# Two-layer decoder on one core: the retention output product with its four plain chunks first

## The chip, the core and the metric

The kernel runs on one core of a Trainium2 chip. The time is the device time of one execution in microseconds (us); the kernel before takes 1469.75 us in the median of three runs (1469.37 to 1470.0). Engines are called as in the profile: PE multiplies matrices (PEld is its loading of weights), DVE is the vector engine, ACT the scalar engine, POOL the general one, SP the one whose queue issues nearly all DMAs.

## The reference, cut to what matters

```python
D_MODEL = 1024; SEQ = 512; DEPTH = 2; RET_HEADS = 4; RET_V_DIM = 256; D_FF = 4096

def hybrid_layer(x, ...):
    z = rmsnorm(x, g_mix) @ w_in            # q, k, v of attention and retention, gates
    ya = sliding_window_sink_attention(aq, ak, av, sinks) @ w_a
    r = chunkwise_retention(rq, rk, rv)
    r = r * lax.rsqrt(jnp.mean(r * r, axis=-1, keepdims=True) + EPS)   # norm of each head
    r = r.reshape(B, S, RET_V) * jax.nn.silu(rg)
    yb = r @ w_b                            # the retention output product, 1024 x 1024
    mixed = sigmoid(ga) * ya + sigmoid(gb) * yb
    x = x + mixed @ w_out                   # 1024 x 1024
    x = x + square(relu(rmsnorm(x, g_mlp) @ w_up)) @ w_down
    return x

x = hybrid_layer(x, ...)                    # twice
return rmsnorm(x, g_final)
```

Everything is fp32. The input is one sequence of 512 tokens.

## The kernel before

**Products.** Activations lie transposed: 128 channels on the partitions, 512 tokens along them. Each fp32 operand is held as two values `hi` and `lo` whose sum it is, and each product is three matmuls (`products`): `hi` by `hi` (L332), weight `hi` by activation `lo` (L333), weight `lo` by activation `hi` (L334). ACT makes `hi` by a copy and DVE makes `lo` by a subtraction, L286 and L287 for weights, L339 and L340 for activations (`split`; L342 and L343 with a scale).

**Weights.** They come as units of 128x1024, in the one order that `unit_order` lists. SP's queue loads a unit into one of three `raw` buffers; ACT and DVE split it into one of three `hi` and `lo` buffers. So `raw` of a later unit is loaded only once DVE has split an older one, and a new `hi` waits until PE has used the older one for the last time.

**Chunks.** A chunk is 128 output channels by 512 tokens in one PSUM bank. A plain chunk takes 24 matmuls of 128x512. A `group` works on four chunks in four banks with the input blocks in the outer loop (96 matmuls, 4 units), `two_chunks` on two banks (48 matmuls, 2 units).

**Block pairs.** `narrow_pair` makes two chunks by a block scheme with fewer multiplications: 4 units (parts), 96 matmuls of 128x256, on sums of the activations' quarters. `sum_input` makes these sums for two pairs of input blocks: four DVE operations of 128x512 (L626, L627, L629, L630) and two splits of 128x1024 into the buffers called `r` (4 activations stacked; `r<-sums` in the profile). A pair's own DVE work is L675 and L678 (adding a partial result out of PSUM) and three calls of its `put`. PSUM banks are reused inside a pair: its last quarter is written into the bank that L675 reads, so it waits for L675. Two further DVE operations for each pair of weights that was not prepared earlier make the weights' sums (L252, L255, L259, L260).

**Stage around the change.** The retention output product (`w_b`) comes in this order: pair 0 and pair 2 (`mixed_pair`, L1238; `put` multiplies by the gate at L1244, and L1247 adds the attention's part for both chunks), then `sum_input` over the first half of the mixed values, then four plain chunks, each evacuated by `put_mixed` (L1218 multiplies, L1219 adds, then a split), then `sum_input` over the second half. In between, `delayed_step` lets one delayed split be issued at steps 2 and 4 of a pair. Then the residual `x` is loaded anew (L1278) into the buffer that held the attention's part, and the product with `w_out` follows: `two_chunks` (L1306; each adds into `x` at L1288) and three pairs (L1296). `next_input` scales and splits the finished chunks of `x` for the product after it (L342, L343).

**Last head.** Each retention head has a norm over 256 channels. Heads 0 to 2 go through `inverse_rms_apart`, head 3 through `inverse_rms` (square root on ACT at L479, reciprocal of 128x512 on DVE at L480). `finish` multiplies by the inverse and by the gate (L1089, L1090), per 128x512.

**What sets the order.** The kernel is written in Tile's language, with `schedule_with_timeline_sim=True`: a planner sets each engine's order of instructions from its own estimate of when their inputs are there. Each engine then works strictly in that order, so an instruction that waits holds up all behind it on its engine.

Of the kernel before, what the change touches and what calls it, by code (L numbers as in the profile page):

```python
# [14 lines left out]
ALU = mybir.AluOpType  # L15
# [3 lines left out]
P = 128  # L19
# [39 lines left out]
def unit_order():  # L59

    def plain(name, *at):
        return [(name, i) for i in range(*at)]

    def pairs(src, *firsts):
        return [("pair", j, part, src) for j in firsts for part in range(4)]

    order = plain("w_in", 26) + plain("w_a", 4) + plain("w_in", 26, 46)
    order += pairs("w_b", 0, 2) + plain("w_b", 4, 8)
    order += plain("w_out", 2) + pairs("w_out", 2, 4, 6)
    for what, q, i in mlp_sequence():  # L70
        if what == "first":
            order += plain("w_up", 4)
        elif what == "pair":
            order += pairs("w_up", 8 * q + 2 * i)
        elif what == "down":
            order += plain("w_down", 8 * q + 2 * i, 8 * q + 2 * i + 2)
        else:
            order += plain("w_down", 8 * q, 8 * q + 8)
    return order
# [43 lines left out]
def view(slot):  # L123
    return slot[0][:, slot[1], :]
# [3 lines left out]
def decoder(ctx, tc, xT, x_first, w_in, w_a, w_b, w_out, w_up, w_down, tables, decay, band, triangles, g_last, out):  # L128
# [207 lines left out]
    def split(hi, lo, src, scale=None):  # L336

        if scale is None:
            nc.scalar.activation(hi, src, AF.Copy)  # L339
            nc.vector.tensor_tensor(lo, src, f32(hi), ALU.subtract)  # L340
        else:
            nc.scalar.activation(hi, src, AF.Copy, scale=scale)  # L342
            nc.vector.scalar_tensor_tensor(lo, src, scale, f32(hi), ALU.mult, ALU.subtract)  # L343
# [259 lines left out]
    def layer_body(layer):  # L603
# [6 lines left out]
        def forms_home():  # L610

            t = slots.four()
            form = t[0].rearrange("p a (b t) -> p (a b) t", t=H).rearrange("p (j k s) t -> p j k s t", k=2, s=2)
            return t, form

        def sum_input(by_form, b, ks):

            (b11, b12), (b21, b22) = ((t[:, :, :H], t[:, :, H:]) for t in b)
            f = [big("sums").rearrange("p a (b t) -> p (a b) t", t=H) for _ in range(2)]
            t1, t2, t3, t4 = f[0][:, 0:2, :], f[0][:, 2:4, :], f[1][:, 0:2, :], f[1][:, 2:4, :]  # L620

            def parts_of_forms(j):
                t = by_form[2 * (j // 2) + ks // 2]
                return [t[:, :, :, s, :] for s in range(2)]

            nc.vector.tensor_tensor(t1, b12, b11, ALU.subtract)  # L626
            nc.vector.tensor_tensor(t2, b22, t1, ALU.subtract)  # L627
            split(*parts_of_forms(0), f[0].rearrange("p (j k) t -> p j k t", k=2))
            nc.vector.tensor_tensor(t3, b22, b12, ALU.subtract)  # L629
            nc.vector.tensor_tensor(t4, b21, t2, ALU.subtract)  # L630
            split(*parts_of_forms(2), f[1].rearrange("p (j k) t -> p j k t", k=2))
# [10 lines left out]
        def form_of(by_form):  # L642
            return lambda j: [by_form[2 * (j // 2) + k // 2][:, j % 2, k % 2, :, :] for k in range(4)]
# [7 lines left out]
        def narrow_pair(pool, step, form, block, put):  # L651
            def multiply(ps, weights, left, moving, start=True):
                hi, lo = weights
                cols = [slice((0 if left else 4 * P) + k * P, (0 if left else 4 * P) + (k + 1) * P) for k in range(4)]
                pairs = [((hi[:, c], lo[:, c]), m if isinstance(m, tuple) else (m[:, 0, :], m[:, 1, :])) for c, m in zip(cols, moving)]
                products(ps, pairs, start, True, not start)

            b, a, e = (bank(pool, "mm")[:, :H] for _ in range(3))
            eu, z = temp("eu"), big("z")
            part = unit("pair", layer)  # L660
            multiply(a, part, True, block(0, 0))
            ins = nc.scalar.activation(b, a, AF.Copy).ins
            step(ins)
            multiply(e, part, False, form(0))
            ins = nc.scalar.activation(eu[:, :H], e, AF.Copy).ins
            step(ins)
            part = unit("pair", layer)
            multiply(b, part, True, form(1), False)
            ins = nc.scalar.activation(eu[:, H:], b, AF.Copy).ins
            step(ins)  # L670
            multiply(a, part, False, block(1, 0), False)
            step(put(0, FIRST, a, z).ins)
            part = unit("pair", layer)
            multiply(b, part, True, form(2), False)
            ins = nc.vector.tensor_tensor(z[:, 1, SECOND], b, eu[:, :H], ALU.add).ins  # L675
            step(ins)
            multiply(e, part, False, block(1, 1), False)
            ins = nc.vector.tensor_tensor(z[:, 0, SECOND], e, eu[:, H:], ALU.add).ins  # L678
            step(ins)
            part = unit("pair", layer)  # L680
            multiply(b, part, True, form(3), False)
            put(slice(0, 2), SECOND, z[:, :, SECOND], z)
            put(1, FIRST, b, z)
            return z
# [324 lines left out]
        class Head:  # L1009
# [70 lines left out]

            def norm(self):
                self.inv = temp("inv")
                (inverse_rms if self.h == 3 else inverse_rms_apart)(self.parts, RET_V, self.inv)

            def finish(self):
                h = self.h
                for e in range(2):
                    z = rg.pop(2 * h + e)
                    nc.vector.tensor_tensor(z, z, self.inv, ALU.mult)  # L1089
                    nc.vector.tensor_tensor(z, self.rr[e], z, ALU.mult)  # L1090
                    hi, lo = slots.one(), slots.one()
                    split(view(hi), view(lo), z)
                    ret[2 * h + e] = (hi, lo)

        def retention(pair):
# [104 lines left out]
        def gate_tile():  # L1200
            c = len(gates)
            two = big("gate")
            nc.sync.dma_start(two, aside[:, c : c + 2, :])
            gate_tiles.append(two)
            gates.extend(two[:, j, :] for j in range(2))
# [18 lines left out]
        rT = [tuple(view(s) for s in ret[k]) for k in range(KD)]  # L1224
        delayed = []

        def delayed_step():
            turn = iter(range(6))

            def step(ins):  # L1230
                now = next(turn)
                if now in (2, 4) and delayed:
                    with tc.issue_after(ins):
                        delayed.pop(0)()

            return step

        def mixed_pair(c):  # L1238

            gate_tile()  # L1240
            two, own = gate_tiles[c // 2], CROSSED[c]

            def put(i, at, src, z):
                return nc.vector.tensor_tensor(two[:, i, at], two[:, i, at], src, ALU.mult)  # L1244

            narrow_pair(ps_aux if c == 0 else ps_mm, delayed_step(), form_of(by_form_r), block_r, put)
            nc.vector.tensor_tensor(two, two, x[:, own : own + 2, :], ALU.add)  # L1247
            delayed.extend(partial(split_mixed, c + i, gates[c + i]) for i in range(2))

# [1 line left out]
            at = slice(tokens * H, tokens * H + H)  # L1251
            return [tuple(m[:, at] for m in rT[CROSSED[k]]) for k in range(4 * half, 4 * half + 4)]

        for c in (0, 2):
            mixed_pair(c)
        all_of(delayed)
        delayed.clear()
        for t, _ in homes_r:
            slots.give(*t[1])
        homes_m = [forms_home(), None, forms_home(), None]  # L1260
        by_form_m = [h and h[1] for h in homes_m]
        sum_input(by_form_m, gate_tiles[:2], 0)
        for c in range(4, KD):
            if c % 2 == 0:
                gate_tile()
            chunk("w_b", layer, rT, put_mixed(c))
        for k in range(KD):
            slots.give(*ret.pop(k))


        homes_m[1::2] = [forms_home() for _ in range(2)]
        by_form_m[:] = [h[1] for h in homes_m]
        sum_input(by_form_m, gate_tiles[2:], 2)


        source = xT if layer == 0 else spill
# [26 lines left out]
            at = slice(tokens * H, tokens * H + H)  # L1303
            return [tuple(m[:, at] for m in mT[k]) for k in range(4 * half, 4 * half + 4)]

        two_chunks("w_out", layer, [mT[k] for k in CROSSED], [put_x(c) for c in range(2)])  # L1306
        for c in range(2, KD, 2):
            pool = ps_mm if c == 4 else ps_aux
            narrow_pair(pool, delayed_step(), form_of(by_form_m), block_m, add_to_x(c))
# [235 lines left out]
def _crossed(cols):  # L1545

    return cols.reshape(KD, P)[list(CROSSED)].reshape(-1)
# [5 lines left out]

def _out_units(w):
    r = np.arange
    units = _units_twos(w[_crossed(r(D))][:, : 2 * P])
    return units + [_swapped(u) if i % 2 else u for i, u in enumerate(_units_chunks(w, 2 * P + r(D - 2 * P)))]


def _ret_units(w):  # L1560
    cols = _crossed(np.arange(D))
    paired = _units_chunks(w[cols], cols[:T])
    return [_swapped(u) if i % 2 else u for i, u in enumerate(paired)] + _units_chunks(w, cols[T:])


def _up_units(w):
# [101 lines left out]
```

## Time and profile before

| | |
|---|---|
| median of three runs | 1469.75 us |
| span of the profiled execution, first to last instruction | 1467.5 us |
| PE busy | 1461.0 us, 7434 matmuls |
| DVE busy | 1161.6 us |
| ACT busy | 814.6 us |
| DMA queues' share of the 16 engines | 42.9% |

The profile gives no time for its own execution but the span; the median lies 2.25 us above it. Busy times say how much an engine had to do, and not whether it was late in a stage. The views used are the share of each engine, the chain of waits that ended last, and the timeline: one row for each instruction, with its start, its duration, the line, what it writes and reads, and in brackets how long the engine stood idle before it. A row with x2 or more holds several instructions one right after the other. Consecutive instructions of an engine overlap by some tens of nanoseconds, so that the time one takes from its engine is the distance of two starts, which is less than its duration.

### The profile page before, as it was taken

The numbers are of one execution on the slowest core, as the hardware profiler recorded it, in microseconds if no ns is written. First come the engines' busy times: TensorE is split into PE (matmuls) and PEld (weight loads), VectorE is DVE, ScalarE is ACT, GpSimd is POOL, SyncE is SP. The second block draws the span as 40 slices with busy tenths as digits, with TensorE's granted clock in tenths as the row PEclk, the third lists the DMA queues.
The fourth block names the chain that finished last, engine by engine and source line by source line (L and its number), as shares of the span: only waits on it lengthen the run. The fifth ranks groups of instructions, "written<-read, shape, count | busy, mean of one in ns | idle before, by whom it ended". The sixth has DMA issues, their size and how long they took to land.

```text
span 1467.5 us, 20166 instructions
## 1 busy us (share of the span) xinstructions
PE 1461.0 (100%) x7434; PEld 1246.4 (85%) x7434; DVE 1161.6 (79%) x1912; ACT 814.6 (56%) x1306; POOL 3.7 (0%) x14
## 2 busy tenths in 40 slices
PE   9999999999999999999999999999999999999998
PEld 7888888888988888888888888888989888888887
DVE  7998778678988787776678977786899877877774
ACT  7657356654684445444456653666547754455544
POOL 0000000000000000000000000000000000000000
PEclk9999999999999999999999999999999999999999
DMA  6423843356443332333543258323654432333373
GB/s 227 134 87 101 280 166 98 104 171 210 130 120 125 101 115 88 107 108 115 165 121 102 86 168 285 107 95 107 191 197 123 144 101 87 125 105 101 108 200 108
DMA packets 73346, 198.65 MB, mean 135 GB/s; under 512 B 8712, under 2 KB 8864, under 8 KB 73248
## 3 DMA queue, kind: packets, MB, share of 16 engines
q1 hardware_dynamic: 72960, 196.84, 42.5%
q8 instruction: 58, 0.95, 0.3%
q10 hardware_dynamic: 288, 0.52, 0.1%
q14 instruction: 40, 0.33, 0.1%
HBM read 173.73 MB, written 20.98 MB: 133 GB/s over the span
## 4 chain that ended last, share of the span: by engine, by line
PE 99%; DVE 0%; issue 0%; POOLq 0%; ACT 0%; DVEq 0%; ACTq 0%
PE mm L334 24%; PE mm L332 23%; PE mm L333 23%; PE mm L1356 11%; PE mm L1357 6%; PE rv L332 2%; PE rv L334 2%; PE rv L333 2%; PE score L864 1%; PE r L332 1%; PE r L334 1%; PE r L333 1%; PE pT L819 0%; PE pv L846 0%; PE pv L845 0%; PE warm L311 0%
## 5 line engine op out<-in xcount | busy, mean ns | idle before, releaser
L333 PE MATMUL mm<-r,hi 128*128 128x512 f32 (+1 forms) x1568 | 572.5, 367 | 0.0
L332 PE MATMUL mm<-r,hi 128*128 128x512 f32 (+1 forms) x1568 | 569.9, 367 | 0.0
L334 PE MATMUL mm<-r,lo 128*128 128x512 f32 (+1 forms) x1568 | 563.9, 367 | 0.2
L286 ACT ACTIVATE hi<-raw 128x1024 fp32r<-128x1024 f32 (+1 forms) x334 | 333.9, 1002 | 377.8 <-PE mm L333 206.9
L287 DVE TENSOR_TENSOR lo<-raw,hi 128x512 fp32r<-128x512 f32 (+1 forms) x335 | 384.3, 1150 | 110.8 <-ACT hi L286 109.4
L334 PEld LDWEIGHTS mm<-r,lo 128*128 128x128 f32 x1568 | 293.6, 188 | 48.8 <-DVE lo L287 1.4
L332 PEld LDWEIGHTS mm<-r,hi 128*128 128x128 f32 x1568 | 294.1, 188 | 46.5 <-ACT r L342 0.2
L333 PEld LDWEIGHTS mm<-r,hi 128*128 128x128 f32 x1568 | 294.3, 188 | 46.0
L1356 PE MATMUL mm<-r,hi 128*128 128x512 f32 x728 | 252.0, 391 | 0.0
L1357 PE MATMUL mm<-r,lo 128*128 128x256 f32 x728 | 200.3, 277 | 0.0
L1356 PEld LDWEIGHTS mm<-r,hi 128*128 128x128 f32 x728 | 136.5, 188 | 28.7 <-ACT mm L1383 0.2
L1357 PEld LDWEIGHTS mm<-r,lo 128*128 128x128 f32 x728 | 136.7, 188 | 3.2 <-DVE lo L287 0.6
L1429 ACT ACTIVATE z<-z 128x512 f32<-128x512 f32 x56 | 32.5, 624 | 51.8 <-DVE z L1409 51.8
L1436 DVE TENSOR_TENSOR x<-x,mm 128x512 f32<-128x512 f32 x56 | 37.7, 686 | 28.1 <-PE mm L334 28.1
L334 PE MATMUL rv<-hi,r 128*128 128x512 f32 x128 | 49.8, 389 | 0.0
L333 PE MATMUL rv<-lo,r 128*128 128x512 f32 x128 | 49.8, 389 | 0.0
L332 PE MATMUL rv<-hi,r 128*128 128x512 f32 x128 | 49.8, 390 | 0.0
L339 ACT ACTIVATE r<-z 128x512 fp32r<-128x512 f32 x64 | 38.5, 619 | 16.3 <-DVE z L1090 16.1
L340 DVE TENSOR_TENSOR r<-z,r 128x512 fp32r<-128x512 f32 x64 | 42.9, 685 | 4.7 <-ACT r L339 4.3
L891 ACT ACTIVATE sm<-sm,st 128x256 f32<-128x256 f32 (+1 forms) x64 | 30.1, 472 | 19.0 <-DVE st L879 18.8
L1409 DVE SCALAR_TENSOR_TENSOR z<-z,rstd 128x512 f32<-128x512 f32 x52 | 35.6, 685 | 0.6
L340 DVE TENSOR_TENSOR r<-sums,r 128x1024 fp32r<-128x1024 f32 x24 | 28.9, 1216 | 0.0
(270 smaller groups left out, 1679.2 us busy)
## 6 DMA issues: line engine op xcount, KB each, us to landing
raw<-w_in_in SPq DMA_DIRECT2D x89, 512.0 KB, 3.6
raw<-w_down_in SPq DMA_DIRECT2D x64, 512.0 KB, 3.6
raw<-w_up_in SPq DMA_DIRECT2D x32, 512.0 KB, 3.9
raw<-w_up_in SPq DMA_DIRECT2D x60, 256.0 KB, 2.9
raw<-w_a_in SPq DMA_DIRECT2D x8, 512.0 KB, 6.5
ahead<-w_b_in SPq DMA_DIRECT2D x8, 512.0 KB, 5.4
park_w_b<-ahead SPq DMA_DIRECT2D x16, 256.0 KB, 5.9
ahead<-w_up_in SPq DMA_DIRECT2D x8, 512.0 KB, 5.7
```

The source lines that it names most:

```text
L286: nc.scalar.activation(hi[:, at], raw[:, at], AF.Copy)
L287: last_low[:] = [nc.vector.tensor_tensor(lo[:, at], raw[:, at], f32(hi[:, at]), ALU.subtract).ins]
L332: nc.tensor.matmul(ps, ah, bh, start=start and i == 0, stop=False, **more)
L333: nc.tensor.matmul(ps, ah, bl, start=False, stop=False, **more)
L334: nc.tensor.matmul(ps, al, bh, start=False, stop=stop and i == n - 1, **more)
L339: nc.scalar.activation(hi, src, AF.Copy)
L340: nc.vector.tensor_tensor(lo, src, f32(hi), ALU.subtract)
L1356: nc.tensor.matmul(both, hi[:, c], m, start=start and k == 0, stop=False, **more)
L1357: nc.tensor.matmul(ps[:, :H], lo[:, c], m[:, 0, :], start=False, stop=k == 3 and start, **more)
L1409: nc.vector.scalar_tensor_tensor(z[:, :, at], z[:, :, at], 0.0, factor, ALU.max, ALU.mult)
L1429: nc.scalar.activation(z[:, i, :], z[:, i, :], AF.Square)
L1436: nc.vector.tensor_tensor(x[:, c, :], x[:, c, :], ps, ALU.add)
```

## The change

The plain half of `w_b` goes first. Its four chunks are no longer made one after the other but as a `group` with the heads' blocks in the outer loop, and their evacuations are put on the list of delayed steps. All four gate tiles are loaded before. Then pair 0 runs, with up to four delayed evacuations issued at its steps 0, 1, 2 and 4, then pair 2, and at the end `sum_mixed(0)`, the sums over the pairs' half; `sum_mixed(2)`, over the plain half, is a delayed step between the two pairs. The order of units follows, `two_chunks` of `w_out` takes the plain half's blocks (4 to 7) first and the pairs' half behind, and the rows of `w_out` are rolled accordingly on the host. The last head's norm takes `inverse_rms_halved`: two square roots of 64x256, one reciprocal of 128x256 and four copies of 64x256. `finish` works on 128x1024, two operations instead of four.

The number and shapes of the matmuls stay as they were. Lines from L1244 on have moved by one: L1244 and L1247 of before are L1243 and L1246 after, L1278 is L1279, L1288 is L1289, L1296 is L1297.

```diff
-    order += pairs("w_b", 0, 2) + plain("w_b", 4, 8)
+    order += plain("w_b", 4, 8) + pairs("w_b", 0, 2)
...
-                (inverse_rms if self.h == 3 else inverse_rms_apart)(self.parts, RET_V, self.inv)
+                (inverse_rms_halved if self.h == 3 else inverse_rms_apart)(self.parts, RET_V, self.inv)
...
+                two = rg_tiles[h]
+                nc.vector.tensor_tensor(two, two, self.inv.unsqueeze(1).broadcast_to([P, 2, T]), ALU.mult)
+                nc.vector.tensor_tensor(two, self.both, two, ALU.mult)
                 for e in range(2):
-                    z = rg.pop(2 * h + e)
-                    nc.vector.tensor_tensor(z, z, self.inv, ALU.mult)
-                    nc.vector.tensor_tensor(z, self.rr[e], z, ALU.mult)
...
-            narrow_pair(ps_aux if c == 0 else ps_mm, delayed_step(), form_of(by_form_r), block_r, put)
+            narrow_pair(ps_aux if c == 0 else ps_mm, delayed_step((0, 1, 2, 4)), form_of(by_form_r), block_r, put)
...
-        for c in (0, 2):
-            mixed_pair(c)
+        for _ in range(4):
+            gate_tile()
...
+        delayed.extend(group("w_b", layer, rT, [put_mixed(c) for c in range(4, KD)]))
+        mixed_pair(0)
+        delayed.append(partial(sum_mixed, 2))
+        mixed_pair(2)
         all_of(delayed)
...
-        sum_input(by_form_m, gate_tiles[:2], 0)
-        for c in range(4, KD):
-            if c % 2 == 0:
-                gate_tile()
-            chunk("w_b", layer, rT, put_mixed(c))
...
-        sum_input(by_form_m, gate_tiles[2:], 2)
+        sum_mixed(0)
...
-        two_chunks("w_out", layer, [mT[k] for k in CROSSED], [put_x(c) for c in range(2)])
+        two_chunks("w_out", layer, [mT[CROSSED[c]] for c in (4, 5, 6, 7, 0, 1, 2, 3)], [put_x(c) for c in range(2)])
```

**DVE ahead of the first unit of `w_out`.** In the names `gate` holds the mixed values, `mm` is a PSUM bank, `lo` the low half of a unit of weights and `r` that of an activation. Before, the rows that lead to the first `lo` of `w_out` (`lo_3241`) begin behind the pairs, beside the plain chunks:

```order
L287 TENSOR_TENSOR lo_3167<-raw_3093,hi_3166 128x1024
L627 TENSOR_TENSOR sums_3152<-gate_3020,sums_3152 128x512
L629 TENSOR_TENSOR sums_3153<-gate_3020,gate_2893 128x512
L287 TENSOR_TENSOR lo_3202<-raw_3127,hi_3201 128x1024
L340 TENSOR_TENSOR r1_77<-gate_3020,r1_77 128x512 x2
L630 TENSOR_TENSOR sums_3153<-gate_3020,sums_3152 128x512
L340 TENSOR_TENSOR r7_83<-sums_3152,r7_83 128x4x256
L1218 TENSOR_TENSOR gate_3162<-mm_3170,gate_3162 128x512
L1218 TENSOR_TENSOR gate_3162<-mm_3205,gate_3162 128x512
L287 TENSOR_TENSOR lo_3241<-raw_3164,hi_3240 128x1024
```

PE has the plain chunks to work on in the meantime. After, the same `lo` is called `lo_3252`. The stretch of DVE that leads to it begins with L675 of pair 0, which waits for PE's last matmul into `mm_3023` (part 3 of pair 0):

```order
L675 TENSOR_TENSOR z_3027<-mm_3023,eu_3026 128x256
L1218 TENSOR_TENSOR gate_2894<-mm_2899,gate_2894 128x512
L626 TENSOR_TENSOR sums_3224<-gate_2892 128x512
L1243 TENSOR_TENSOR gate_2888<-gate_2888,z_3027 128x2x256
L287 TENSOR_TENSOR lo_3146<-raw_3069,hi_3145 128x1024
L1219 TENSOR_TENSOR gate_2894<-gate_2894,x_75 128x512
L1243 TENSOR_TENSOR gate_2888<-gate_2888,mm_3023 128x256
L287 TENSOR_TENSOR lo_3172<-raw_3106,hi_3171 128x1024
L627 TENSOR_TENSOR sums_3224<-gate_2894,sums_3224 128x512
```

It goes on with:

```order
L629 TENSOR_TENSOR sums_3225<-gate_2894,gate_2892 128x512
L1246 TENSOR_TENSOR gate_2888<-gate_2888,x_75 128x1024
L287 TENSOR_TENSOR lo_3208<-raw_3143,hi_3207 128x512
L340 TENSOR_TENSOR r1_77<-gate_2894,r1_77 128x512
L630 TENSOR_TENSOR sums_3225<-gate_2894,sums_3224 128x512
L1243 TENSOR_TENSOR gate_2890<-gate_2890,mm_3165 128x256
L340 TENSOR_TENSOR r3_79<-sums_3224,r3_79 128x4x256
L678 TENSOR_TENSOR z_3168<-mm_3166,eu_3167 128x256
L287 TENSOR_TENSOR lo_3252<-raw_3169,hi_3251 128x1024
```

The evacuations of the group (L1218, L1219), its sums and splits and the pairs' own work now stand together here, 17 rows from L675 to L678 ahead of `lo_3252`.

**PE at the start of `w_out`.** Before, the last quarter of pair 2 (`mm_3022<-r5_81`) follows matmuls of the first plain chunk (`mm_3170`):

```order
L333 MATMUL mm_3170<-r9_85,hi_3095 128x512
L334 MATMUL mm_3170<-r9_85,lo_3096 128x512
L332 MATMUL mm_3170<-r9_85,hi_3095 128x512
L332 MATMUL mm_3022<-r5_81,hi_3061 128x256
L333 MATMUL mm_3022<-r5_81,hi_3061 128x256
L334 MATMUL mm_3022<-r5_81,lo_3062 128x256
```

After, it stands behind 26 matmuls of `w_out`, the first of which (`mm_3324<-r0_76,hi_3251`) follow the third part of pair 2 directly; the matmul with `lo_3252` is the fifth row of `w_out`. The quarter begins here:

```order
L334 MATMUL mm_3325<-r1_77,lo_3252 128x512
L332 MATMUL mm_3324<-r2_78,hi_3283 128x512
L333 MATMUL mm_3324<-r2_78,hi_3283 128x512
L332 MATMUL mm_3164<-r5_81,hi_3207 128x256
L333 MATMUL mm_3164<-r5_81,hi_3207 128x256
L334 MATMUL mm_3164<-r5_81,lo_3208 128x256
```

It moved from the middle of `w_b` into `w_out`, whose later blocks are made from its result.

**DVE behind that quarter.** Its last matmul frees the first row here (L1243); the rows are, in order, the multiplication by the gate, a weight's `lo`, the adding of the attention's part (L1246), another weight's `lo`, two sums for `sum_mixed(0)`, two sums of weights, and the two splits of the last two chunks, whose results `r6_82` the product waits for:

```order
L1243 TENSOR_TENSOR gate_2890<-gate_2890,mm_3164 128x256
L287 TENSOR_TENSOR lo_3328<-raw_3247,hi_3327 128x1024
L1246 TENSOR_TENSOR gate_2890<-gate_2890,x_75 128x1024
L287 TENSOR_TENSOR lo_3357<-raw2_3281,hi_3356 128x1024
L627 TENSOR_TENSOR sums_3306<-gate_2890,sums_3306 128x512
L629 TENSOR_TENSOR sums_3307<-gate_2890,gate_2888 128x512
L259 TENSOR_TENSOR raw3_3395<-raw_3247,raw_3249 128x512
L260 TENSOR_TENSOR raw3_3395<-raw2_3281 128x512
L340 TENSOR_TENSOR r6_82<-gate_2890,r6_82 128x512 x2
```

**PE there.** The rows that use what DVE makes: `r6_82` is one of the pair's chunks, `r4_80` the split form of `sums_3306`, and the matmul of L333 reads the split's `lo`:

```order
L333 MATMUL mm_3387<-r0_76,hi_3327 128x256
L334 MATMUL mm_3387<-r0_76,lo_3328 128x256
L332 MATMUL mm_3324<-r6_82,hi_3283 128x512
L332 MATMUL mm_3325<-r6_82,hi_3283 128x512
L332 MATMUL mm_3387<-r6_82,hi_3356 128x256
L332 MATMUL mm_3388<-r4_80,hi_3327 128x256
L332 MATMUL mm_3386<-r4_80,hi_3356 128x256
L333 MATMUL mm_3324<-r6_82,hi_3283 128x512
L334 MATMUL mm_3324<-r6_82,lo_3284 128x512
```

Before, the second unit of `two_chunks` was broken up in a similar way for the last plain chunk (`r3_79`), whose values come straight from a bank by two operations and a split:

```order
L333 MATMUL mm_3389<-r2_78,hi_3329 128x256
L332 MATMUL mm_3326<-r3_79,hi_3275 128x512
L332 MATMUL mm_3327<-r3_79,hi_3275 128x512
L334 MATMUL mm_3389<-r2_78,lo_3330 128x256
L332 MATMUL mm_3389<-r2_78,hi_3329 128x256
L333 MATMUL mm_3389<-r2_78,hi_3329 128x256
L334 MATMUL mm_3389<-r2_78,lo_3330 128x256
L333 MATMUL mm_3326<-r3_79,hi_3275 128x512
L334 MATMUL mm_3326<-r3_79,lo_3276 128x512
```

After, what stands there hangs on a pair's last quarter.

More of the change, by code (lines that the diff above doesn't have):

```diff
@@ L1082, in norm @@
                 self.inv = temp("inv")
-                (inverse_rms if self.h == 3 else inverse_rms_apart)(self.parts, RET_V, self.inv)
+                (inverse_rms_halved if self.h == 3 else inverse_rms_apart)(self.parts, RET_V, self.inv)
             def finish(self):
                 h = self.h
+                two = rg_tiles[h]
+                nc.vector.tensor_tensor(two, two, self.inv.unsqueeze(1).broadcast_to([P, 2, T]), ALU.mult)
+                nc.vector.tensor_tensor(two, self.both, two, ALU.mult)
                 for e in range(2):
-                    z = rg.pop(2 * h + e)
-                    nc.vector.tensor_tensor(z, z, self.inv, ALU.mult)
-                    nc.vector.tensor_tensor(z, self.rr[e], z, ALU.mult)
                     hi, lo = slots.one(), slots.one()
-                    split(view(hi), view(lo), z)
+                    split(view(hi), view(lo), rg.pop(2 * h + e))
                     ret[2 * h + e] = (hi, lo)
@@ L1225, in layer_body, with delayed_step @@
         delayed = []
-        def delayed_step():
+        def delayed_step(at=(2, 4)):
             turn = iter(range(6))
@@ L1231, in step @@
                 now = next(turn)
-                if now in (2, 4) and delayed:
+                if now in at and delayed:
                     with tc.issue_after(ins):
@@ L1252, in block_r, with sum_mixed @@
             return [tuple(m[:, at] for m in rT[CROSSED[k]]) for k in range(4 * half, 4 * half + 4)]
-        for c in (0, 2):
-            mixed_pair(c)
+        for _ in range(4):
+            gate_tile()
+        homes_m = [None] * 4
+        by_form_m = [None] * 4
+        def sum_mixed(ks):
+            for i in (ks // 2, ks // 2 + 2):
+                homes_m[i] = forms_home()
+                by_form_m[i] = homes_m[i][1]
+            sum_input(by_form_m, gate_tiles[ks : ks + 2], ks)
+        delayed.extend(group("w_b", layer, rT, [put_mixed(c) for c in range(4, KD)]))
+        mixed_pair(0)
+        delayed.append(partial(sum_mixed, 2))
+        mixed_pair(2)
         all_of(delayed)
         delayed.clear()
+        for k in range(KD):
+            slots.give(*ret.pop(k))
         for t, _ in homes_r:
             slots.give(*t[1])
-        homes_m = [forms_home(), None, forms_home(), None]
-        by_form_m = [h and h[1] for h in homes_m]
-        sum_input(by_form_m, gate_tiles[:2], 0)
-        for c in range(4, KD):
-            if c % 2 == 0:
-                gate_tile()
-            chunk("w_b", layer, rT, put_mixed(c))
[L1267 to L1272, printed above, removed]
-        sum_input(by_form_m, gate_tiles[2:], 2)
+        sum_mixed(0)
         source = xT if layer == 0 else spill
@@ L1555, in _out_units @@
     r = np.arange
-    units = _units_twos(w[_crossed(r(D))][:, : 2 * P])
+    rows = np.roll(_crossed(r(D)), D // 2)
+    units = _units_twos(w[rows][:, : 2 * P])
     return units + [_swapped(u) if i % 2 else u for i, u in enumerate(_units_chunks(w, 2 * P + r(D - 2 * P)))]
@@ L1562, in _ret_units @@
     paired = _units_chunks(w[cols], cols[:T])
-    return [_swapped(u) if i % 2 else u for i, u in enumerate(paired)] + _units_chunks(w, cols[T:])
+    return [_swapped(u) if i % 2 else u for i, u in enumerate(paired)] + _units_group(w, cols[T:])
 def _up_units(w):
```

## The prediction

> **What bounds the kernel now.** I read the shares of the engines first, then the clock, then the chain that ended last, and at last the timelines of PE and DVE around the change.
>
> ```profile
> PE 1461.0 (100%) x7434; PEld 1246.4 (85%) x7434; DVE 1161.6 (79%) x1912; ACT 814.6 (56%) x1306; POOL 3.7 (0%) x14
> ...
> PE 99%; DVE 0%; issue 0%; POOLq 0%; ACT 0%; DVEq 0%; ACTq 0%
> core 0: 1467.5 us, clock 1.000
> ```
>
> PE is busy from end to end at the full clock, and the chain is PE's own. The 7434 matmuls keep their shapes, so the change gains only where PE waits now, and it loses wherever it makes PE wait. How fast PE goes is the distance of starts, first at 128x512, then at 128x256:
>
> ```profile
> 315.74 0.39 PE L334 MATMUL mm<-r,lo 128*128 128x512 f32 x1
> ...
> 318.24 0.39 PE L333 MATMUL mm<-r,hi 128*128 128x512 f32 x1
> ...
> 318.93 0.28 PE L333 MATMUL mm<-r,hi 128*128 128x256 f32 x1
> ...
> 319.99 0.28 PE L333 MATMUL mm<-r,hi 128*128 128x256 f32 x1
> ```
>
> Eleven steps in 2.50 us make 0.227 us for a matmul of 512 columns, nine in 1.06 make 0.118 for one of 256. Stretches longer than these steps add up to PE's waits. In this stage there are two:
>
> ```profile
> 379.63 0.28 PE L333 MATMUL mm<-r,hi 128*128 128x256 f32 x1
> 379.91 0.39 PE L334 MATMUL mm<-r,lo 128*128 128x256 f32 x1
> 380.13 0.28 PE L332 MATMUL mm<-r,hi 128*128 128x256 f32 x1
> ...
> 391.21 0.75 PE L334 MATMUL mm<-r,lo 128*128 128x256 f32 x2
> 391.80 0.28 PE L332 MATMUL mm<-r,hi 128*128 128x256 f32 x1
> ```
>
> The first holds 0.50 us for two steps, the second 0.59: 0.26 + 0.35 = 0.61 us too long. The chain shows layer 1 with the same cause as layer 0, DVE's `lo` behind a split:
>
> ```profile
> 390.30 1.23 DVE lo L287
> 391.57 0.39 PE mm L334
> ...
> 1118.20 1.23 DVE lo L287
> 1119.47 0.38 PE mm L334
> ```
>
> So 2 x 0.6 = 1.2 us is the most that a better order of this stage can gain. What it can lose hangs on DVE. Busy time by stretch (PE, PEld, DVE, ACT, in us with the counts in brackets): the pairs of `w_b`, the plain chunks, the same plain chunks in layer 1:
>
> ```profile
> 312.00:344.00 32.00, 32.00 (x223) 29.78 (x223) 22.53 (x31) 15.90 (x25) 0.00 (x0) 1.00 0.75 247
> 344.00:361.00 17.00, 17.00 (x77) 14.08 (x76) 17.00 (x23) 8.62 (x11) 0.00 (x0) 1.00 0.68 233
> ...
> 1078.00:1095.00 17.00, 17.00 (x77) 14.08 (x75) 16.96 (x25) 6.49 (x10) 0.00 (x0) 1.00 0.59 201
> ```
>
> DVE idles 9.5 us beside the pairs, and not at all beside the plain chunks, where it catches up with the sums, splits and evacuations while PE has matmuls that need none of them. The change puts these matmuls first and the pairs, with all that hangs on them, last.
>
> **The change part by part.** DVE's prices are distances of starts in a stretch without idle time:
>
> ```profile
> 343.17 0.28 PE L334 MATMUL mm<-r,lo 128*128 128x256 f32 x1
> ...
> 343.49 0.42 DVE L1244 TENSOR_TENSOR gate<-gate,mm 128x256 f32<-128x256 f32 x1 [2.48 <-PE mm L334]
> 343.94 1.23 DVE L1247 TENSOR_TENSOR gate<-gate,x 128x1024 f32<-128x1024 f32 x1
> 345.08 1.22 DVE L287 TENSOR_TENSOR lo<-raw,hi 128x1024 fp32r<-128x1024 f32 x1
> 346.22 0.68 DVE L627 TENSOR_TENSOR sums<-gate,sums 128x512 f32<-128x512 f32 x1
> 346.82 0.69 DVE L629 TENSOR_TENSOR sums<-gate 128x512 f32<-128x512 f32 x1
> ...
> 388.70 0.42 DVE L675 TENSOR_TENSOR z<-mm,eu 128x256 f32<-128x256 f32 x1
> 389.04 0.74 DVE L343 SCALAR_TENSOR_TENSOR r<-x,r 128x512 fp32r<-128x512 f32 x1
> ```
>
> From 343.94 to 345.08 is 1.14 us for 1024 columns, from 346.22 to 346.82 is 0.60 for 512, from 388.70 to 389.04 is 0.34 for 256. From the start of a pair's last matmul (343.17) to DVE's first row on its bank (343.49) is 0.32. ACT's prices:
>
> ```profile
> 346.94 1.06 ACT L339 ACTIVATE r<-sums 128x1024 fp32r<-128x1024 f32 x1 [0.52 <-DVE sums L627]
> ...
> 356.08 1.13 ACT L339 ACTIVATE r<-gate 128x512 fp32r<-128x512 f32 x2
> ...
> 361.06 0.61 ACT L339 ACTIVATE r<-gate 128x512 fp32r<-128x512 f32 x1
> ...
> 371.70 0.37 ACT L662 ACTIVATE mm<-mm 128x256 f32<-128x256 f32 x1 [2.68 <-PE mm L334]
> ```
>
> ACT takes 1.06 us for 1024 columns, 0.61 for 512 and 1.13 for two of them, so 0.52 from start to start, and 0.37 for 256. L627 ends at 346.90 and ACT starts at 346.94: 0.04 from one engine to the next.
>
> *Wait A, the first unit of `w_out`.* Let s be the start of the last matmul into `mm_3023` (part 3 of pair 0). DVE starts L675 at s + 0.32. The order shows 17 rows from there to `lo_3252`: four of 256 columns (1.36), nine of 512 (5.40; `lo_3208` is one, and the 2x256), four of 1024 (4.56), together 11.32. `lo_3252` is there 1.22 + 0.04 later, at s + 12.90. PE has until then the other two parts of pair 0 and three of pair 2, 85 steps of 0.118, and four of 0.227: s + 10.94. PE waits 1.96 us. If DVE is already behind at L675, which the evacuations ahead of it make possible, it waits more.
>
> *Wait B, the chunks of pair 2.* Now s is the start of the last matmul of the quarter that stands in `w_out`. DVE needs 0.32, then L1243 (0.34), three rows of 1024 (3.42), four of 512 (2.40), then the split `r6_82` (0.68 + 0.04): s + 7.20. ACT's half of `r4_80` is there at 0.32 + 0.34 + 3.42 + 0.68 + 0.04 + 1.06 + 0.04 = s + 5.90. PE has one step of 0.118, ten of 0.227, twelve of 0.118, two of 0.227 and three of 0.118: 4.61. It waits 1.5 us at `r4_80` and 1.1 at `r6_82`, together 2.59.
>
> *Wait C, the next pair's copy.* ACT holds the copy that releases the pair's third step behind the split of the finished `x`. DVE comes to that `x` (second L1289) six rows of 512 and two of 1024 behind the start of `r6_82`'s split, s + 6.48 + 5.88 = s + 12.36; plus 0.68 + 0.04, on ACT 0.52 + 0.52 + 0.37, and 0.04: s + 14.53. PE gets there at 7.20 + 10 x 0.227 + 33 x 0.118 = s + 13.36. It waits 1.17 us.
>
> *Behind that* the order is nearly the old one, so the old 0.6 us should stay, and the late start adds little: I take 0.3 more, between a gain of 0.6 (both old waits vanish) and a loss of 1 (about one more `lo`, 1.23).
>
> *The last head.* The reciprocal halves:
>
> ```profile
> 300.29 3.35 DVE L480 RECIPROCAL inv<-inv 128x512 f32<-128x512 f32 x1 [1.58 <-ACT inv L479]
> ...
> L469 DVE RECIPROCAL own<-own x2: 1752/1752/1752, 424.3 to 1152.2; 128x256 f32<-128x256 f32 x2
> ...
> PE warm L311 <- DVE ones L306: 1.0, 1, 1.0
> ```
>
> The second row is the halved form, which the norm ahead of the MLP has already (durations of its two executions in ns): 1752 for 3355 ns, 1.60 us less on DVE. The third is all that the list of PE's waits for the whole program holds, so PE did not wait for this norm: it ends at 303.64, and `w_b` begins 15 us later. I cost it at nothing; the gate chunks in between hide it, and would hide a loss of the same size (the additional small instructions on ACT). `finish` takes 2 x 1.14 for 4 x 0.60: nothing.
>
> *The group.* 96 x 0.227 = 21.8 us of PE's time, as for four chunks. DVE has only weights to split there, and this is the room it loses later.
>
> *Queues.* On SP three reloads of `x` now stand ahead of pair 2's loads, since the plain half is done with its part of the buffer earlier.
>
> ```profile
> raw<-park_w_b SPq DMA_DIRECT2D x8, 256.0 KB, 3.8
> ...
> x<-xT_in SPq DMA_DIRECT2D x8, 256.0 KB, 6.2
> raw<-w_out_in SPq DMA_DIRECT2D x4, 512.0 KB, 3.5
> ```
>
> Pair 2's second part has 58 steps of 0.118 = 6.8 us from the release of its buffer to its use, less 1.06 for ACT: a landing in 3.8 is in time, one in 6.2 is 0.5 late. The later loads have about 5.3 us, against 3.5 to 6.2. Between 0 and about 1 us each at three places, I take 0, nearer to the rows of their own kind. The four gate loads come earlier, beside work that does not need them.
>
> *Sum.* 1.96 + 2.59 + 1.17 + 0.3 = 6.0 us for a layer, 12.0 for two: a span of 1479.5 after 1467.5. The median lies 2.25 above the span, so 1481.75; I say 1482.
>
> *The clock.* [...] At the start PE ran ten matmuls slowly:
>
> ```profile
> 1.04 4.63 PE L311 MATMUL warm<-ones 128*128 128x512 f32 x10 [1.04 <-DVE ones L306]
> 5.47 1.25 PE L332 MATMUL mm<-r,hi 128*128 128x512 f32 x4
> ```
>
> That is 0.443 us each, 0.216 more than later, 2.2 us in all. [...]
>
> **The rivals.** *DVE keeps up (not slower).* In the order of before, the second unit of `two_chunks` is broken up in the same manner, from 368 to 372 us. PE and DVE (first and third figure) were both busy throughout:
>
> ```profile
> 368.00:372.00 4.00, 4.00 (x25) 3.50 (x24) 4.00 (x5) 1.32 (x3) 0.00 (x0) 1.00 0.38 121
> ```
>
> This speaks for it. It decides where the 17 rows take 9.4 us instead of 11.3, and where B's chain shrinks from 7.2 to 4.6. Against it: all the durations are measured ones, and nothing in the diff shortens an operation. The time would be 1469.75 less 0 to 1.2: 1469.
>
> *A gain beyond the measurement.* What a measurement tells from no change is 0.2%, 2.9 us. PE's waits in this stage are 1.2, so only matmuls that themselves go faster could do it. If the 2 x 192 matmuls of `w_b`'s pairs fell from 0.118 to half of 0.227, that is 1.7: 1466.8.
>
> *Late loads.* The three places take their full 1 us each in both layers: 1482 + 6 = 1488. For it the 6.2 us of `x`, against it that loads issued early have slack.
>
> [...]
>
> **How the numbers follow.** The forecast has 0.74, late loads 0.10, the slowed clock 0.05, DVE keeping up 0.08, the gain 0.03. Within the forecast the bounds are: B alone, with A and C covered, 2 x (2.59 - 0.6) = 4.0 over before, 1473.7; and with three landings half late, 1485. Its own range is 1474 to 1486. To leave out no more than 2 in 10 the range of all goes from 1473.5 to 1489. Faster by over 0.2% is the gain alone (0.03), within it DVE keeping up (0.08), slower the rest (0.89).
>
> **What would show it.** In the timeline of after, PE should have a gap of about 2 us at the fifth matmul of `w_out` in both layers, ended by `lo` of L287, and about 2.6 around the splits L339 and L340 of pair 2's chunks, with DVE busy without a break from the end of pair 0 on. PE's busy time should hardly move and the MLP stages not at all. If PE runs through both places, DVE was not the bound there, and the forecast is wrong; if the gaps end with a DMA, the loads are the cause.

## The result

The changed kernel takes 1489.12 us in the median (four runs, 1487.53 to 1491.64) against 1469.56 for the kernel before (1469.13 to 1470.0): a ratio of 1.0135, 95% interval 1.0121 to 1.0149. That is 19.6 us slower. The forecast was 1482, its range ended at 1489.0, and so the direction was right and the size too small by 7.

The profiled execution (1487.53 us, span 1485.7) is 18.2 us longer than the one of before. Its page and the list of what PE waited for (us in total, times, longest) have:

```profile
PE 1464.6 (99%) x7434; PEld 1245.9 (84%) x7434; DVE 1157.9 (78%) x1896; ACT 818.0 (55%) x1316; POOL 3.7 (0%) x14
...
PE mm L334 <- DVE lo L287: 6.4, 7, 1.8
PE mm L332 <- ACT own L468: 3.2, 2, 1.6
PE mm L332 <- ACT r L339: 2.0, 2, 1.0
PE mm L333 <- DVE r L340: 1.6, 2, 0.8
PE mm L332 <- ACT eu L665: 1.1, 1, 1.1
PE warm L311 <- DVE ones L306: 1.0, 1, 1.0
```

Where this list had one row before, it has six, and all but the last are new. PE's busy time grew by only 3.6 us. The timeline of PE shows the waits at the start of `w_out` in layer 0 (the bracket is the idle time ahead of a row):

```profile
358.79 0.39 PE L333 MATMUL mm<-r,hi 128*128 128x512 f32 x1
360.96 0.73 PE L334 MATMUL mm<-r,lo 128*128 128x512 f32 x2 [1.79 <-DVE lo L287]
...
371.07 0.28 PE L334 MATMUL mm<-r,lo 128*128 128x256 f32 x1
371.31 1.18 PE L332 MATMUL mm<-r,hi 128*128 128x512 f32 x3
373.47 0.50 PE L332 MATMUL mm<-r,hi 128*128 128x256 f32 x2 [0.98 <-ACT r L339]
374.79 0.50 PE L333 MATMUL mm<-r,hi 128*128 128x512 f32 x1 [0.82 <-DVE r L340]
375.13 0.39 PE L334 MATMUL mm<-r,lo 128*128 128x512 f32 x1
...
380.98 0.28 PE L334 MATMUL mm<-r,lo 128*128 128x256 f32 x1
382.39 0.39 PE L332 MATMUL mm<-r,hi 128*128 128x256 f32 x1 [1.13 <-ACT eu L665]
...
430.78 0.28 PE L334 MATMUL mm<-r,lo 128*128 128x256 f32 x1
432.66 0.39 PE L332 MATMUL mm<-r,hi 128*128 128x256 f32 x1 [1.60 <-ACT own L468]
```

From 371.07 to 375.13 there are 4.06 us for steps that take 1.15 at PE's plain pace: 2.9 us lost, 2.2 of them ahead of the two rows with a bracket, the rest in steps that came slower than the plain ones. The others are 1.3 at 380.98 and 1.76 at 430.78; the one behind 358.79 is 1.95 and hangs on DVE, whose timeline answers to the stretch shown of before, now without a break:

```profile
348.40 0.42 DVE L675 TENSOR_TENSOR z<-mm,eu 128x256 f32<-128x256 f32 x1 [0.24 <-PE mm L334]
348.75 0.68 DVE L1218 TENSOR_TENSOR gate<-mm,gate 128x512 f32<-128x512 f32 x1
...
359.37 0.41 DVE L678 TENSOR_TENSOR z<-mm,eu 128x256 f32<-128x256 f32 x1
359.70 1.21 DVE L287 TENSOR_TENSOR lo<-raw,hi 128x1024 fp32r<-128x1024 f32 x1
```

If one adds up by how much PE's starts lie further apart than its plain steps, and takes off the same for the kernel before, the stretch from `w_b` to the end of `w_out` costs 6.3 us in layer 0 and 6.2 in layer 1, 12.5 together. The start of the MLP, from 420 and from 1140 us on, costs about 3 in each layer, 6.0 together. The rest of the program is 0.3 shorter. The sum of the forecast, 12.0, was for the first of these; the second was not in it.

### The profile page after: what moved, and what is told of

The parts are those of the page before. It is cut to its first block, busy times and chain, and to the rows that moved or that the text cites. A ratio compares the mean times of both kernels' runs of the same rounds, so it can differ in the third digit from the quotient of the medians.

```text
span 1485.7 us, 20159 instructions
## 1 busy us (share of the span) xinstructions
PE 1464.6 (99%) x7434; PEld 1245.9 (84%) x7434; DVE 1157.9 (78%) x1896; ACT 818.0 (55%) x1316; POOL 3.7 (0%) x14
## 5 line engine op out<-in xcount | busy, mean ns | idle before, releaser
L333 PE MATMUL mm<-r,hi 128*128 128x512 f32 (+1 forms) x1568 | 572.9, 367 | 1.6 <-DVE r L340 1.6
L333 PEld LDWEIGHTS mm<-r,hi 128*128 128x128 f32 x1568 | 294.5, 188 | 48.0 <-DVE r L340 2.0
L333 PE MATMUL rv<-lo,r 128*128 128x512 f32 x128 | 49.8, 389 | 0.0
L340 DVE TENSOR_TENSOR r<-z,r 128x512 fp32r<-128x512 f32 x64 | 42.4, 685 | 8.5 <-ACT r L339 8.5
L340 DVE TENSOR_TENSOR r<-sums,r 128x1024 fp32r<-128x1024 f32 x24 | 29.0, 1215 | 0.0
```

The lines of the kernel that those rows point to most:

```text
L333: nc.tensor.matmul(ps, ah, bl, start=False, stop=False, **more)
```

## The experiments

The theory after the result had two parts: DVE's rows make PE wait around `w_out`, as forecast; and one row that moved on ACT makes it wait at the start of the MLP. Rivals were that the norm of the last head has a share, that the loss at the MLP only passes on the lateness of `w_out`, that loads come late, and that the group, with its evacuations all at the end, is to blame and not the place of the pairs.

**The last head's norm alone**, in the kernel before:

```diff
-                (inverse_rms if self.h == 3 else inverse_rms_apart)(self.parts, RET_V, self.inv)
+                (inverse_rms_halved if self.h == 3 else inverse_rms_apart)(self.parts, RET_V, self.inv)
...
+                nc.vector.tensor_tensor(two, two, self.inv.unsqueeze(1).broadcast_to([P, 2, T]), ALU.mult)
+                nc.vector.tensor_tensor(two, self.both, two, ALU.mult)
```

> The kernel before with the last head's norm halved and finish on 128x1024, nothing else. Theory (DVE and ACT late around the pairs, the norm off the path): the same time within 1 us, about 1469.5. Rival (the norm's extra ACT work delays the gate chunks): 2 to 4 us slower, with a wait of PE near 300 us.

It took 1469.15 us against 1469.26 (ratio 1.0000, 0.9990 to 1.0009). The norm is off the path, as costed.

**The reordering alone**: the changed kernel with that part taken back.

```diff
-                (inverse_rms_halved if self.h == 3 else inverse_rms_apart)(self.parts, RET_V, self.inv)
+                (inverse_rms if self.h == 3 else inverse_rms_apart)(self.parts, RET_V, self.inv)
```

> The changed kernel with the last head's norm and finish as before, so the reordering alone. Theory: the same waits at the same places, 1487 to 1490. Rival (the norm has a part in the loss): 2 to 4 us below the changed kernel.

1488.41 us (1487.27 to 1490.47), ratio 1.0134 (1.0119 to 1.0149), with the same waits at the same places. All of the loss belongs to the order.

**The root first on ACT.** In the changed kernel ACT starts the MLP like this:

```profile
424.58 1.04 ACT L339 ACTIVATE r<-sums 128x1024 fp32r<-128x1024 f32 x1
429.28 1.06 ACT L286 ACTIVATE hi<-raw 128x1024 fp32r<-128x1024 f32 x1 [3.66 <-issue]
430.36 1.28 ACT L468 ACT_TABLE_LOAD   x1
431.65 0.95 ACT L468 ACTIVATE own<-ssq,x 64x256 f32<-64x256 f32 x2
432.63 0.37 ACT L662 ACTIVATE mm<-mm 128x256 f32<-128x256 f32 x1
```

And in the kernel before:

```profile
418.70 1.05 ACT L339 ACTIVATE r<-sums 128x1024 fp32r<-128x1024 f32 x1
419.76 1.28 ACT L468 ACT_TABLE_LOAD   x1
423.35 0.95 ACT L468 ACTIVATE own<-ssq,x 64x256 f32<-64x256 f32 x2 [2.31 <-PE ssq L464]
424.33 1.06 ACT L286 ACTIVATE hi<-raw 128x1024 fp32r<-128x1024 f32 x1
```

Before, ACT loads the table for the square root and then waits for the norm's sum. After, a weight's copy stands ahead of it. ACT is idle for 3.66 us before that copy, and only then come the table (1.28 us) and the root. The bracket names no releaser ("issue" means that the profile shows nothing it waited for); that the copy waits for PE's last use of its buffer is inferred from a matmul of PE that ends 0.09 us ahead of it. PE waits for the root: its row at 432.66 starts 0.06 us after the root's end. The edit ties that copy of weights behind the root (`nullcontext` elsewhere):

```diff
-                    nc.scalar.activation(hi[:, at], raw[:, at], AF.Copy)
+                    with tc.issue_after(last_root[0]) if paired and order[i][2:5:2] == (4, "w_up") and order[i][3] == 2 else nullcontext(): nc.scalar.activation(hi[:, at], raw[:, at], AF.Copy)
```

> The changed kernel with one edge on ACT: the copy into hi of the third part of the first w_up pair goes behind the square root of the MLP's norm, as it stands before. Theory (the two waits at 431 and 451 us come from that row's place on ACT): PE's waits of 1.6 us on the root and the 0.8 us some 20 us later vanish in both layers, the three places around w_out stay; about 6 us less, 1483. Rival (the start of the MLP is late because w_out is late): the waits stay or go elsewhere, 1488 to 1490.

1484.49 us (1482.49 to 1486.09), ratio 1.0105 (1.0090 to 1.0120), 4.6 below the changed kernel. No wait on the root is left in the list of what PE waited for:

```profile
PE mm L334 <- DVE lo L287: 5.1, 5, 1.8
PE mm L332 <- ACT eu L665: 2.0, 1, 2.0
PE mm L332 <- ACT r L339: 2.0, 2, 1.0
PE mm L333 <- DVE r L340: 1.6, 2, 0.8
PE warm L311 <- DVE ones L306: 1.0, 1, 1.0
```

The start of the MLP costs about 0.6 and 0.1 us more than before, not 3. The waits around `w_out` stay, and they are now nearly all of the loss.

**The root last, in the kernel before.** The converse, with the norm's end called behind the last unit of the group and tied behind the copy:

```diff
+        def root():
+            with tc.issue_after(copied[0]): rms_mlp.finish()
...
-                rms_mlp.finish()
...
+            return {0: lambda: (rms_mlp.prepare(), sum_input(by_form, scaled_pair(0, g_mlp), 0)), 1: at1, 3: root}
```

> The kernel before with one edge: on ACT the MLP's root goes behind the copy into hi of the third part of the first w_up pair, the order that the changed kernel has (the norm's last matmul moves by three rows on PE). Theory (that row's place costs by itself, whatever went before): PE waits 1.6 us on the root and about 1 us more some 20 us later in both layers, 5 to 6.5 us in all, 1474 to 1476. Rival (it costs only where the stage is late already): as before, 1469.3.

1474.51 us (1473.91 to 1474.92) against 1469.31, ratio 1.0034 (1.0022 to 1.0047): 5.2 us from the place of the root and its table load behind that copy, in a kernel that is otherwise not late. (The norm's last matmul moved on PE as well, so this converse is less pure than the edge alone.) Behind 425.49 its PE loses 1.53 us to the root, where the changed kernel loses 1.76:

```profile
425.49 0.28 PE L334 MATMUL mm<-r,lo 128*128 128x256 f32 x1
427.14 0.38 PE L332 MATMUL mm<-r,hi 128*128 128x256 f32 x1 [1.37 <-ACT own L468]
```

So the loss at the MLP does not pass on the lateness of `w_out`; that rival fell from both sides.

**Without the attention's part**: the changed kernel without L1219 and L1246, so that `mixed` lacks its first term.

```diff
-                nc.vector.tensor_tensor(m, m, mixed[CROSSED[c]], ALU.add)
...
-            nc.vector.tensor_tensor(two, two, x[:, own : own + 2, :], ALU.add)
```

> The changed kernel without the attention's part: neither the four additions of 128x512 at L1219 nor the two of 128x1024 at L1246 (the output lacks sigmoid(ga) * ya). DVE has 4.7 us less per layer. By its order the row on ACT stands behind the root again as well. Theory (DVE is the bound at the start of w_out): the wait at the first lo of w_out falls from 1.95 to below 0.5 us, that at r6 and r4 from 2.4 to about 1.3, and with the MLP's 3 us the time falls by about 12 to 1477. Rival (late loads, or the split quarter of pair 2 itself): the two places keep their waits and only the MLP's go, 1483.

1473.75 us (1472.92 to 1474.47), 15.4 below the changed kernel and more than expected. The wait at the first `lo` fell to 1.0 us and not below 0.5, since the planner put two splits of 512 columns (L340) into the room: from L675 to that `lo` DVE is still full, 348.95 to 359.38 in its timeline. That is 10.43 us for 11.30, and the wait became shorter by about as much, 0.94.

```profile
348.95 0.42 DVE L675 TENSOR_TENSOR z<-mm,eu 128x256 f32<-128x256 f32 x1 [0.24 <-PE mm L334]
...
359.38 1.22 DVE L287 TENSOR_TENSOR lo<-raw,hi 128x1024 fp32r<-128x1024 f32 x1
```

The waits at `r4` and `r6` vanished altogether, and the root stands first on ACT again. That the first wait follows DVE's rows is shown by it. For the waits at `r4` and `r6` it is not: L1246 also stands in the chain from the quarter to these splits, and the order moved too.

**Chunk by chunk, still first**, on top of the root first (the host's order of these units follows):

```diff
-        delayed.extend(group("w_b", layer, rT, [put_mixed(c) for c in range(4, KD)]))
+        for c in range(4, KD): chunk("w_b", layer, rT, put_mixed(c))
```

> As the changed kernel with the root first on ACT (the run before this one with 1484.5), but the plain half is made chunk by chunk, each evacuated beside the next, still ahead of the pairs. Theory (the waits follow from DVE's rows and their order, not from the group): the order still has 15 rows between L675 and the first lo of w_out, four of 256, six of 512 and five of 1024 columns, 10.7 us for 11.3, so the first wait falls from 1.95 only to 1.3 us, and the two at r4 and r6 fall by about the one lo that now comes ahead (1.1); the time falls by 1.3 to 4 us, 1480.5 to 1483. Rival (the group's late evacuations are the cause): the first wait vanishes and the time falls by 6 or more.

1484.50 us (1482.70 to 1485.71), the same as with the group (1484.49) and not the 1480.5 to 1483 that I expected. The first wait is 1.29 us in both layers, as summed from the 15 rows:

```profile
359.31 0.39 PE L333 MATMUL mm<-r,hi 128*128 128x512 f32 x1
360.83 0.50 PE L334 MATMUL mm<-r,lo 128*128 128x512 f32 x1 [1.13 <-DVE lo L287]
```

The equal times hide two differences. Added up as above, this stage loses 11.6 us to waits against 13.0 with the group, so they fell by 1.4, the low end of what I expected. But PE's granted clock was near half for a stretch in each layer of this profile (0.52 from 375 to 378, 0.51 from 1119 to 1122) and in one layer of the other (0.59 from 384 to 387), and the slower steps cost 2.7 us against 1.5. So the group may cost up to some 1.4 us, within one profile of each kernel; the 6 or more of the rival it does not.

**The group last**, in the kernel before (the last two gate tiles are loaded ahead of it, and the host's order of its units follows):

```diff
-            chunk("w_b", layer, rT, put_mixed(c))
+        all_of(group("w_b", layer, rT, [put_mixed(c) for c in range(4, KD)]))
```

> The kernel before with the pairs first as they were, and the plain half made as a group behind them. Theory (DVE has too little cover at the start of w_out as soon as four evacuations, or a pair, end right ahead of it): PE waits at the splits of the last plain chunks, 2 to 4 us a layer, 1473 to 1477. Rival (only the pairs at the end cost time): as before, 1469.3.

1471.36 us (1470.84 to 1472.05), ratio 1.0014 (1.0004 to 1.0023): 2.2 us slower, less than expected. PE runs through the splits of the plain chunks and waits only 0.5 and 0.6 us at the next pair. A plain chunk needs two operations and a split from its bank to its use, and four of them at the end are covered nearly whole; the pair at the end of the changed kernel is not.

**The old order of blocks in `w_out`**, on top of the root first:

```diff
-        two_chunks("w_out", layer, [mT[CROSSED[c]] for c in (4, 5, 6, 7, 0, 1, 2, 3)], [put_x(c) for c in range(2)])
+        two_chunks("w_out", layer, [mT[k] for k in CROSSED], [put_x(c) for c in range(2)])
...
-    rows = np.roll(_crossed(r(D)), D // 2)
+    rows = _crossed(r(D))
```

> As the changed kernel with the root first on ACT (1484.5), but the two chunks of w_out take their blocks in the old order, the pairs' half first. Theory (what PE waits for is the split of pair 2's chunks, 7.2 us behind the quarter): these blocks are now wanted about 2 us earlier, so the wait there grows to about 4 us a layer, 1487 to 1490. Rival (the first lo alone decides): no change, 1484.5.

1489.65 us (1487.75 to 1490.65), 5.2 above the same with the new order. The time is in the range, but not for my reason: in both layers PE loses 3.0 us at the first split that it needs, of one of pair 0's chunks (`r2`), with further waits of 1.2 to 2.4 us behind it. Much of the time is the clock, which stands at half for about 6.8 us a layer in this profile (granted 0.50 from 363 to 366 and from 1110 to 1116): the slower steps there cost about 4.9 us in all, against 1.5 in the run with the new order. Without them the waits of this stage grew by only about 1.6 us. The new order of blocks is the better one for the change, and does not make up for it.

## Why the forecast was right in its direction and too small

- *What bounds the kernel.* Right: PE had 1.2 us to gain here, and the change gained none of it.
- *Wait A, 1.96 us.* Measured 1.95 in both layers; DVE reached the `lo` 11.30 us behind L675, summed as 11.32.
- *Wait B, 2.59.* Measured 2.9 and 2.8. In layer 0 DVE's first weight `lo` started 0.2 us later than summed (0.54 us behind L1243 in its timeline, not 0.34).
- *Wait C, 1.17.* Measured 1.3 in layer 0, on the copy as forecast. In layer 1 the mechanism did not hold: the copy (L665) stands ahead of the split of `x` (L342) there, and what PE waited for was a weight's `lo`, 0.9. The sum took one layer's order for both, and that the second came out near it is luck.

```profile
1117.76 0.36 ACT L665 ACTIVATE eu<-mm 128x256 f32<-128x256 f32 x1
1118.02 0.72 ACT L342 ACTIVATE r<-x 128x512 fp32r<-128x512 f32 x1
```

- *Behind that, 0.3.* Taking A to C off the 6.3 and 6.2 us leaves 0.2 and 0.5. So the stage cost 12.5 against 12.0.
- *The last head, nothing.* Right, by the run of it alone.
- *The group, nothing by itself.* Right to within 1.4 us: chunk by chunk takes the same time, with somewhat less waiting and more slowed clock.
- *Late loads.* Nearly none: one wait of 0.36 us on a load (DVE's L252 at 366.27) in this stage of layer 0.
- *"The MLP stages not at all".* This is the step that failed. The sum had no term for the start of the MLP, and the prediction shows no row of ACT there. A copy of weights moved ahead of the norm's root: 3.0 us a layer in the profile, 4.6 us in all when it is taken back, 5.2 when it is put into the kernel before. Why the planner moved it no run shows.
- *The clock.* The sum had no term for a slowed clock; the chance of 0.05 for it was the author's estimate, and the profile of the kernel before shows no fall of the clock at a gap (1.00 from 6 to 1462 us). The runs showed drops in the kernel with the root first and in the two built on it, at gaps of 1.1 to 3.0 us, and the clock probably had a share here too. The four runs of the changed kernel have mean granted clocks of 0.999, 0.997, 0.995 and 0.999 beside 1487.53, 1489.27, 1491.64 and 1488.98 us; those of before have 0.999 or 1.000. The profile is that of the shortest run, so the last 1.6 us up to the median were not seen in it. That they are the clock's is argued from these pairs and from the other profiles below, and not shown for this kernel itself; the fourth run, 1.45 us above the first at the same 0.999, does not speak for it.
- *The 2.25 us from the span to the time.* Too much: in one and the same run it is 1.8 (1487.53 against 1485.7).

From the summed 1481.75 to the measured 1489.12 the steps are then 0.5 around `w_out`, 6.0 at the MLP, 0.3 and 0.4 less for the rest of the program and the last point, and 1.6 from the profiled run to the median.

With the root first, the time is 1484.49, 2.5 us over the forecast. Its profile, a run of 1484.73, shows where this comes from: about 1.0 us more waiting around `w_out` (in layer 0 one of 2.1 behind 381.17, where 1.2 was summed), about 0.7 at the MLP, and 1.5 in steps slowed by the clock, which was granted at 0.59 from 384 to 387 and 0.84 from 387 to 390.

## What to carry to other kernels

Where an engine of a full pipeline waits can be summed by hand from distances of starts in the trace and the order of rows: the first wait came out within 0.02 us, in two kernels, the later ones of the forecast within about 0.3. But the comparison of orders has to cover every engine and every layer, and to go on to the next place where all meet: here one row on the least busy of the three, with a table load behind it, cost a quarter to a third of the loss. In this kernel, work with many steps from its last matmul to its next use belonged early, and what needs two operations and a split belonged last.

## What the runs showed of the hardware

PE's granted clock fell to about half at gaps of PE, in the profiles of the kernel with the root first and of the two built on it. The chunk-by-chunk kernel, layer 1, has its longest gap, 2.2 us, at 1115.59. Its timeline of PE, and by stretch the busy times (PE, PEld, DVE, ACT, POOL) with the granted clock behind them:

```profile
1115.59 0.28 PE L334 MATMUL mm<-r,lo 128*128 128x256 f32 x1
1117.89 0.38 PE L332 MATMUL mm<-r,hi 128*128 128x256 f32 x1 [2.03 <-ACT eu L665]
...
1118.58 0.41 PE L334 MATMUL mm<-r,lo 128*128 128x256 f32 x1
...
1121.78 0.36 PE L332 MATMUL mm<-r,hi 128*128 128x256 f32 x1
1121.98 0.28 PE L333 MATMUL mm<-r,hi 128*128 128x256 f32 x1
1122.10 0.28 PE L334 MATMUL mm<-r,lo 128*128 128x256 f32 x1
```

```profile
1110.00:1116.00 6.00, 5.87 (x42) 5.34 (x40) 5.05 (x7) 2.12 (x2) 0.00 (x0) 1.00 0.24 83
1116.00:1119.00 3.00, 1.11 (x7) 1.11 (x8) 2.36 (x4) 2.67 (x5) 0.00 (x0) 0.92 0.00 0
1119.00:1122.00 3.00, 3.00 (x16) 3.00 (x16) 2.22 (x3) 1.71 (x4) 0.00 (x0) 0.51 0.60 183
1122.00:1125.00 3.00, 3.00 (x27) 3.00 (x27) 2.23 (x5) 1.44 (x2) 0.00 (x0) 1.00 0.00 0
```

From 1118.58 to 1121.78 PE took fifteen steps of 0.213 us, where 0.118 is the plain one: 1.4 us lost. The first slow one starts 0.7 us after PE is busy again (1117.89). The length of a single gap does not tell whether the clock falls: one of 1.95 us (wait A) had no such drop behind it in any profile here, and of the two of 3.0 us in the kernel with the old order of blocks one had it (layer 0, the first three rows) and the other had not (layer 1, the last two):

```profile
360.00:363.00 3.00, 0.43 (x1) 0.43 (x2) 3.00 (x6) 1.24 (x2) 0.00 (x0) 0.80 0.66 220
363.00:366.00 3.00, 3.00 (x10) 2.42 (x10) 3.00 (x4) 0.00 (x0) 0.00 (x0) 0.50 0.50 176
366.00:369.00 3.00, 3.00 (x14) 2.71 (x13) 2.93 (x6) 1.06 (x1) 0.00 (x0) 0.56 0.27 87
...
1098.00:1101.00 3.00, 0.74 (x3) 0.65 (x4) 3.00 (x6) 0.92 (x1) 0.00 (x0) 1.00 0.73 212
1101.00:1104.00 3.00, 3.00 (x20) 2.56 (x19) 3.00 (x5) 0.00 (x0) 0.00 (x0) 1.00 0.43 164
```

Nor does the idle time within such a stretch of 3 us: from 1098 to 1101 PE is idle here for 2.26 us and the clock stays at 1.00, and in the kernel with the root first it is idle for 1.97 from 381 to 384 and the clock is 0.59 in the stretch behind. What decides it these runs do not show.
